# Dividing the softmax behind the product with v instead of ahead of it

## The chip, the core and the metric

The kernel runs on one core of a Trainium2 chip. The metric is the device time of one execution in microseconds, the median of several runs; less is better. The core has five engines that matter here, each with a queue of its own: TensorE (PE in the profile; PEld is its weight load), VectorE (DVE), ScalarE (ACT), GpSimd (POOL) and SyncE (SP), which issues the transfers. TensorE writes PSUM, eight banks of 128 x 512 float32; everything else lies in SBUF.

## What is computed

A two-layer encoder over 512 tokens of width 1024. Each layer is a half-step feed-forward block, a token mixer and another feed-forward block. The mixer makes q, k, v and u by one projection, runs windowed attention (8 heads of 64, 2 key/value heads, blocks of 128 queries) beside a state-space branch, normalizes both results and projects them out. The part that is changed is the end of the attention:

```
s = q k^T / 8 + bias, masked to |i - j| <= 128
m = max(max(s), sink);  p = exp(s - m)
denom = sum(p) + exp(sink - m)
p = p / denom
o = p v
attn = o;  rms_norm(attn) goes into the output projection
```

## The kernel before

Activations are kept with channels on the partitions and the 512 tokens in columns. Products of float32 data are made as three products of rounded parts (`mm3`, L214 to L218): high by high, high by low, low by high. ScalarE rounds the high part of each weight chunk (L199), VectorE, for some chunks GpSimd, subtracts to get the low part (L202).

The mixer (L762) is a list of small steps in the order of `ORDER` (L42 to L46), emitted one after the other. Attention has eight units, a block n of 128 queries with a key/value head kv; unit 0 is (0, 0), unit 1 is (0, 1), and so on. For each unit:

- `as` (a_scores, L954): the scores of four heads, bias and maximum on VectorE (L971), exp with its row sums on ScalarE (L978), the sink's term (L979).
- `an` (a_norm, L982): VectorE adds the sink's term (L988), takes the reciprocal (L989) and multiplies the four heads' p by it, one instruction per head (L993). Queries lie on the partitions here, so the factor is one number per partition.
- `ao` (a_out, L995): TensorE turns p by transposes of 128 x 128, four to a PSUM bank (L1001); VectorE (L1004) or ScalarE (L1006) copies each bank out.

For each block n there is then `pv` (a_pv, L1011): the product with v, one product for each key block and kv (L1016); a float32 product shows as two records in the trace. The two kv use different halves of the array's columns and write different partitions of one bank o. Behind it VectorE multiplies o by the gain of the norm (L1025, result f), ScalarE rounds f to its high part (L1027) and squares o (L1028), VectorE makes the low part (L1030), and GpSimd, for n = 3 VectorE, adds up the squares (L1032, L1033). The second output projection (`wa`, from L1148, by `wout`) needs all four blocks' high and low parts; the rstd of the norm (`rstd_a`, L329) needs the sums of squares. The first output projection, of the state-space branch, is the steps `ws0` to `ws7`, twelve products of 128 x 512 each; its sums are made by L1069 and added to x by L1071. The feed-forward block behind the mixer rounds x by L281 and L287 first.

The list ends with `... as7 ws6 an7 ao7 ao6 pv2 ws7 pv3`. Emission sets the dependences, but not alone the order within an engine's queue: the kernel asks that queues be planned when it is compiled (`TCKW`, L38), and the trace shows steps out of the order of the list. The preparation of the second layer's state-space tables (`s5_steps`, L518, in the trace L456 to L641) is emitted behind the first mixer, and some of it runs during the mixer's end.

PSUM banks are handed out in turn, the one that was given back first being next (`bank`, L146). SBUF slots of 128 x 512 come from 16 blocks of four (`slot`, L101).

Of the kernel before, what the change touches and what calls it, by code (L numbers as in the profile page):

```python
# [11 lines left out]
AF = mybir.ActivationFunctionType  # L12
# [17 lines left out]

# column indices in the table of per-partition gains
GC_FFN1, GC_MIX, GC_ATT, GC_SSM, GC_FFN2, GC_BGLU, GC_L = 0, 8, 16, 20, 24, 32, 36
# [7 lines left out]
N_CONST = 640  # L40
# order of the parts of the token mixer (see Emit.mixer)
ORDER = """  # L42
# [3 lines left out]
""".split()  # L46
# weight chunks of the mixer, by halves, whose low parts GpSimd makes
POOL_SPLIT = {("u", 0, 0), ("u", 0, 1), ("u", 2, 0), ("q", 0, 0), ("q", 0, 1), ("q", 2, 1), ("glu", 0, 1),
              ("ws", 0, 1), ("ws", 4, 0), ("wa", 0, 1), ("wa", 4, 1)}
# low parts of q, by head of the group and half, that GpSimd makes  # L50
POOL_Q = ((2, 1), (3, 1))
# tiles of the output whose sums in the mixer VectorE makes, of the first and of the second product
ADD_V = ((0, 7), (5, 7))
# tiles of x, by first and number, as they are loaded
STARTX = ((0, 1), (1, 1), (2, 2), (4, 2), (6, 2))


def weight_chunks():
    """Chunks of stationary blocks in the order of their use: (kind, args, columns)."""
    out = []  # L60
    for l in range(L):
        for which in (0, 1):
            if which == 1:
                out += [("u", (l, 0), 2048), ("u", (l, 2), 2048), ("kv", (l,), 2048),
                        ("q", (l, 0), 2048), ("q", (l, 2), 2048)]
                out += [("glu", (l,), 2048), ("ws", (l, 0), 2048), ("ws", (l, 4), 2048),
                        ("wa", (l, 0), 2048), ("wa", (l, 4), 2048)]
            for f0, nf in FGROUPS:
                for f in range(f0, f0 + nf):
                    out.append(("gu", (l, which, f), 2048))  # L70
                for dp in range(4):
                    out.append(("dn", (l, which, f0, nf, dp), 2 * nf * P))
    return out


class Emit:
# [22 lines left out]

# [1 line left out]
    def slot(self, n=1, r=False):  # L101
# [56 lines left out]

# [1 line left out]
    def set_bg(self, gen, steps, points):  # L160
        """Spread gen, of about so many steps, over so many points of the main work."""
        self.bg = gen
        self.bg_at, self.bg_n, self.bg_rate = 0, 0, steps / points
# [13 lines left out]

# [1 line left out]
    def w_load(self, upto):  # L179
# [39 lines left out]

# [1 line left out]
    def const(self, n):  # L221
# [5 lines left out]
    def setup(self, st):  # L227
        """Constants, the input, and the first chunk of weights, in the order in which the first products want them."""
        I, V, S, SP, Gp = self.I, self.V, self.S, self.SP, self.G
# [44 lines left out]

# [1 line left out]
    def x_hi(self, d, st):  # L276
        """The rounded part of h = x * gain for tile d."""
        if d % 4 == 0:
            st["blk"] += [self.slot(4, True), self.slot(4, True)]
        hi, lo = (x[:, (d % 4) * T:(d % 4 + 1) * T] for x in st["blk"][-2:])  # L280
        self.S.activation(hi.bitcast(F32R), self.x[d], AF.Copy, scale=self.gains[:, st["g"] + d:st["g"] + d + 1])  # L281
        st["h"].append((hi, lo))

    def x_lo(self, d, st):
        """The rest of h."""
        hi, lo = st["h"][d]
        self.V.scalar_tensor_tensor(lo.bitcast(F32R), self.x[d], self.gains[:, st["g"] + d:st["g"] + d + 1], hi,  # L287
                                    op0=ALU.mult, op1=ALU.subtract)
# [6 lines left out]
    def x_acc(self, d, st, eng):  # L295
        """The running sum of squares."""
        if d:
# [25 lines left out]
    def rstd_a(self, acc, n, w=T):  # L323
        """Column sums of acc -> 1/sqrt(mean + eps), as columns of 128 tokens."""
        V = self.V
# [15 lines left out]
    def rstd_b(self, s, w=T):  # L341
        """The columns as one row of tokens, the same on each partition."""
        b = self.bank()
# [7 lines left out]

# [1 line left out]
    def ffn(self, st, after, tail=None):  # L353
# [65 lines left out]

# [1 line left out]
    def bias_steps(self):  # L421
# [27 lines left out]

# [1 line left out]
    def cmul(self, eng, o, a, b, t, conj=False):  # L451
        """o = a * b (or conj(a) * b), pairs of (re, im)."""
        M, A, B = ALU.mult, ALU.add, ALU.subtract
# [9 lines left out]
    def exp_parts(self, x, w, R):  # L463
        """exp(x) = 2**k * (1 + em): returns (em, 2**k) as tiles of width w."""
        V = self.V
# [18 lines left out]
    def sincos(self, th, w, R):  # L484
        """(cos(th) - 1, sin(th)) with th reduced to [-pi, pi] and then halved."""
        V = self.V
# [31 lines left out]
    def s5_steps(self, l):  # L518
# [60 lines left out]
        yield  # L579
        # powers 0..8  # L580
        tmp = self.slot()
# [20 lines left out]

        # input matrices, as they are and turned back by one chunk
        def g16(x):
# [13 lines left out]
        yield  # L618
        # phasors of 1, 2, 4, .. chunks, backward ones conjugate, of modulus 1
        rho = R()  # L620
# [8 lines left out]
        for k in range(5):  # L629
# [13 lines left out]
            yield  # L643
        # tables over the chunks, 16 groups at a time
        for hf in range(2):
# [34 lines left out]
        yield  # L680
        # output maps, input maps and the taps inside a chunk, 4 groups at a time
        ks = self.slot(3)
# [70 lines left out]

# [1 line left out]
    def proj(self, w, m, h, bank):  # L755
# [6 lines left out]
    def mixer(self, l, st, after):  # L762
# [5 lines left out]

        # u, with the tokens of a chunk apart: (j, c) for t = 8 c + j
        ud = self.dram.tile([4, P, T], F32, name=f"ud{l}")  # L770
# [34 lines left out]

        # state-space pieces, a quarter of the groups at a time
        tabs, Y = {}, {}
# [62 lines left out]
        def s_out(q):  # L870
# [14 lines left out]
            if q % 2 == 0:  # L885
                Y[gh] = [self.slot(), self.slot()]
            # rows (group parity, c); columns (j, group pair, channel)
            for jh in range(2):
# [58 lines left out]

        # attention
        ga = self.gains[:, gl + GC_ATT:gl + GC_ATT + 4]
# [32 lines left out]
        def a_norm(n, kv):  # L982
            k0, k1 = at[n]["k"]
            nk = (k1 - k0) * P
            sm = at[n]["sm"]
# [3 lines left out]
            V.reciprocal(den[:, c4], den[:, c4])  # L989
            for i in range(4):  # L990
                hd = kv * 4 + i
                p = at[n]["p"][kv][:, i * T:i * T + nk]
                V.tensor_scalar(p, p, den[:, hd:hd + 1], None, op0=M)  # L993

# [16 lines left out]
        def a_pv(n):  # L1011
            k0, k1 = at[n]["k"]
            o = self.bank()
            for kb in range(k0, k1):
# [3 lines left out]
            for kv in range(2):  # L1018
                self.free(*at[n][kv])
            # rows (kv, dh); columns (head of the group, token)  # L1020
            if not abuf:
                abuf.extend([self.slot(4, True), self.slot(4, True)])
            cs = slice(n * T, (n + 1) * T)
            f, q = self.slot(), self.slot()
            V.tensor_tensor(out=f.rearrange("p (i t) -> p i t", i=4), in0=o.rearrange("p (i t) -> p i t", i=4),  # L1025
                            in1=ga.rearrange("p (i o) -> p i o", o=1).to_broadcast([P, 4, P]), op=M)
            S.copy(abuf[0][:, cs].bitcast(F32R), f)  # L1027
            S.activation(q, o, AF.Square)  # L1028
            self.bfree(o)
            V.tensor_tensor(out=abuf[1][:, cs].bitcast(F32R), in0=f, in1=abuf[0][:, cs], op=B)  # L1030
            eng = V if n == 3 else Gp
            eng.tensor_tensor(out=q[:, 0:256], in0=q[:, 0:256], in1=q[:, 256:512], op=A)  # L1032
            eng.tensor_tensor(out=acc_a[:, n * P:(n + 1) * P], in0=q[:, 0:P], in1=q[:, P:2 * P], op=A)  # L1033
            self.free(f, q, at[n]["sm"])

        # back to channels on the partitions, and the activation
        z = [None] * 4
# [121 lines left out]
    def final(self, st):  # L1159
        """The last two tiles of the last product, the last norm and the output, half of the tokens at a time."""  # L1160
        V, S, Gp = self.V, self.S, self.G
# [68 lines left out]

# [1 line left out]
def _tiles(w, cols):  # L1232
    """w: (K, N); the 128-column blocks of w[:, cols] as [128, m, k, 128]."""
    k = w.shape[0] // P
    m = len(cols) // P
    return w[:, cols].reshape(k, P, m, P).transpose(1, 2, 0, 3)
# [42 lines left out]
def _bucket(rel):  # L1279
    """Bucket of each relative distance (a constant of the shapes)."""  # L1280
    half, exact = 16, 8
# [81 lines left out]
```

## Time and profile before

| | us |
|---|---|
| median of 3 runs | 1935.28 |
| lowest and highest run | 1933.37, 1935.31 |
| span of the profiled execution | 1932.9 |
| PE busy in the span | 1859.6 (96%) |
| DVE, ACT, POOL busy | 1138.8, 627.4, 698.0 |

The span runs from the first to the last instruction of one profiled execution; that execution's own time is not listed apart from its span. The median of the runs is 2.4 us more than the span, for what lies around it.

How to read the profile: a line of a view names the engine, the source line, the operation and the tiles. A timeline gives start and length of merged runs of the same instruction, and in brackets how long the engine had waited and for whom. The distance between two starts on TensorE is what an instruction costs there, since the records of neighbours overlap.

### The profile page before, as it was taken

To read this page: it belongs to the slowest core of one execution; us is meant where nothing else is said; L and a number is where in the kernel's file an instruction comes from. 1 tells how busy PE (TensorE), PEld (TensorE's weight loads), DVE (VectorE), ACT (ScalarE), POOL (GpSimd) and SP (SyncE) were. 2 spreads that over 40 slices of the span, in tenths; PEclk is the share of its full clock that TensorE was granted. 3 is DMA by queue.
4 is the path that set the end of the run, shared out by engine and by line. 5 is a ranking of instruction groups with operands and counts; after the bars stand their busy time and mean duration, and the time that the engine had idled before them with its cause. 6 is when DMAs were issued, how large, how long until landed. Compare 5 with 4: busy or idle time off the path is not lost. (4 is left out here: it accounts for less than half of the span.)

```text
span 1932.9 us, 23810 instructions
## 1 busy us (share of the span) xinstructions
PE 1859.6 (96%) x9416; PEld 1506.9 (78%) x9416; DVE 1138.8 (59%) x1747; ACT 627.4 (32%) x955; POOL 698.0 (36%) x586
## 2 busy tenths in 40 slices
PE   8999999996999999999999999999969999999997
PEld 6888888875667888888878888888747678888886
DVE  8645545569889634355674453436797773434435
ACT  5223223321743323223332222224227342222223
POOL 2049999235133015093483351103341330201102
PEclk9999999997999999999999999999979999999998
DMA  5533434576111233233333244424640122232321
GB/s 201 164 120 121 160 124 157 160 239 214 50 67 46 107 109 120 99 131 115 108 136 111 99 135 129 138 93 154 219 170 23 51 83 107 88 106 80 109 97 45
DMA packets 86233, 231.13 MB, mean 120 GB/s; under 512 B 31160, under 2 KB 38504, under 8 KB 70376
## 3 DMA queue, kind: packets, MB, share of 16 engines
q1 hardware_dynamic: 84888, 228.51, 35.0%
q8 instruction: 74, 1.21, 0.3%
q10 hardware_dynamic: 1232, 1.09, 0.2%
q14 instruction: 39, 0.32, 0.1%
HBM read 201.11 MB, written 34.75 MB: 122 GB/s over the span
## 5 line engine op out<-in xcount | busy, mean ns | idle before, releaser
L217 PE MATMUL psum<-blk,whi 128*128 128x512 f32 (+1 forms) x2446 | 952.9, 390 | 7.7 <-DVE blk L287 7.6
L216 PE MATMUL psum<-blk,whi 128*128 128x512 f32 (+1 forms) x2446 | 952.4, 392 | 7.5 <-ACT blk L281 6.3
L218 PE MATMUL psum<-blk,wlo 128*128 128x512 f32 (+1 forms) x2446 | 950.6, 389 | 0.9 <-DVE wlo L202 0.7
L217 PEld LDWEIGHTS psum<-blk,whi 128*128 128x128 f32 x2446 | 460.4, 188 | 106.2 <-DVE blk L287 12.8
L216 PEld LDWEIGHTS psum<-blk,whi 128*128 128x128 f32 x2446 | 460.8, 188 | 104.9 <-ACT blk L281 6.5
L218 PEld LDWEIGHTS psum<-blk,wlo 128*128 128x128 f32 x2446 | 460.3, 188 | 96.2 <-DVE wlo L202 1.1
L199 ACT CAST whi<-raw 128x1024 fp32r<-128x1024 f32 (+1 forms) x310 | 303.4, 1027 | 680.1 <-PE psum L217 466.6
L202 DVE TENSOR_TENSOR wlo<-raw,whi 128x1024 fp32r<-128x1024 f32 (+1 forms) x288 | 417.5, 1484 | 38.1 <-ACT whi L199 28.2
L385 DVE TENSOR_TENSOR blk<-psum,blk 128x512 f32<-128x512 f32 x88 | 60.6, 691 | 346.0 <-PE psum L218 343.6
L411 POOL TENSOR_TENSOR xtile<-xtile,blk 128x512 f32<-128x512 f32 x64 | 91.1, 1424 | 375.8 <-DVE blk L409 358.4
L409 DVE SCALAR_TENSOR_TENSOR blk<-psum,blk 128x512 f32<-128x512 f32 x94 | 64.9, 690 | 213.5 <-PE psum L218 203.2
L384 ACT ACTIVATE blk<-blk 128x512 f32<-128x512 f32 x88 | 55.3, 632 | 301.8 <-DVE blk L382 296.8
L701 POOL TENSOR_TENSOR blk<-blk,blk 128x512 f32<-128x512 f32 x64 | 85.4, 1346 | 92.0 <-PE psum L714 51.4
L382 DVE TENSOR_TENSOR blk<-psum,blk 128x512 f32<-128x512 f32 x88 | 60.2, 688 | 88.2 <-PE psum L218 85.4
L299 POOL TENSOR_TENSOR blk<-blk,blk 128x512 f32<-128x512 f32 x29 | 45.0, 1553 | 155.1 <-ACT blk L292 154.3
L202 POOL TENSOR_TENSOR wlo<-raw,whi 128x1024 fp32r<-128x1024 f32 x22 | 61.1, 2785 | 106.6 <-ACT whi L199 65.8
L702 POOL TENSOR_TENSOR blk<-blk,blk 128x512 f32<-128x512 f32 x64 | 85.8, 1343 | 27.5 <-PE psum L714 14.3
L704 POOL TENSOR_TENSOR blk<-blk,blk 128x512 f32<-128x512 f32 x49 | 80.2, 1642 | 2.4
L389 DVE TENSOR_TENSOR blk<-blk,blk 128x512 fp32r<-128x512 f32 x88 | 75.4, 859 | 0.7 <-ACT blk L388 0.7
L287 DVE SCALAR_TENSOR_TENSOR blk<-xtile,consts,blk 128x512 fp32r<-128x512 f32 x48 | 57.1, 1205 | 11.0 <-ACT blk L281 11.0
L1071 POOL TENSOR_TENSOR xtile<-xtile,blk 128x512 f32<-128x512 f32 x24 | 33.2, 1404 | 70.2 <-DVE blk L1069 63.7
L299 POOL TENSOR_TENSOR blk<-blk 128x512 f32<-128x512 f32 x13 | 20.5, 1574 | 99.0 <-ACT blk L292 98.8
(234 smaller groups left out, 1337.5 us busy)
## 6 DMA issues: line engine op xcount, KB each, us to landing
raw<-w SPq DMA_DIRECT2D x123, 1024.0 KB, 4.8
raw<-w SPq DMA_DIRECT2D x32, 896.0 KB, 4.6
fd<-blk SPq DMA_DIRECT2D x32, 256.0 KB, 2.8
ed<-blk SPq DMA_DIRECT2D x32, 256.0 KB, 3.4
blk<-ed SPq DMA_DIRECT2D x32, 256.0 KB, 6.3
blk<-fd SPq DMA_DIRECT2D x32, 256.0 KB, 5.2
tb<-blk SPq DMA_DIRECT2D x12, 512.0 KB, 2.9
blk<-tb SPq DMA_DIRECT2D x24, 256.0 KB, 5.8
```

What stands on the lines that cost most here:

```text
L199: self.S.copy(hi[:, c], raw[:, c])
L202: eng.tensor_tensor(out=lo[:, c], in0=raw[:, c], in1=hi[:, c].bitcast(F32), op=ALU.subtract)
L216: t.matmul(out, wh, xh, start=start, stop=False)
L217: t.matmul(out, wh, xl, start=False, stop=False)
L218: t.matmul(out, wl, xh, start=False, stop=stop)
L299: eng.tensor_tensor(out=acc, in0=acc, in1=sq, op=ALU.add)
L389: V.tensor_tensor(out=lo.bitcast(F32R), in0=s, in1=hi, op=ALU.subtract)
L409: V.scalar_tensor_tensor(t, ps, 0.5, R, op0=ALU.mult, op1=ALU.mult)
L411: (V if last else self.G).tensor_tensor(out=self.x[d], in0=self.x[d], in1=t, op=ALU.add)
L701: Gp.tensor_tensor(out=full(o), in0=mat(a), in1=pwo(w, 0), op=M)
L702: Gp.tensor_tensor(out=full(t), in0=mat(b), in1=pwo(w, 1), op=M)
L704: Gp.tensor_tensor(out=o, in0=o, in1=t, op=sg)
```

## The change

`a_norm` keeps the sum and the reciprocal, and no longer multiplies p. `a_out` turns the undivided p. `a_pv` first spreads the reciprocals: ScalarE copies the eight columns of block n to a tile rd, in which each number stands 64 times side by side; four transposes put them into a bank db, where rows are (kv, channel) and columns are (head, token); ScalarE copies the bank back to rd. Behind the product VectorE multiplies o by rd into rd, and the product with the gain is made from rd, by GpSimd for n = 0, 1, 2 and by VectorE for n = 3. The square is now emitted ahead of the rounding of f. Nothing else is changed (the rest of the diff takes comments out).

```
 def a_norm(n, kv):
-    k0, k1 = at[n]["k"]
-    nk = (k1 - k0) * P
     sm = at[n]["sm"]
     c4 = slice(kv * 4, kv * 4 + 4)
     den, t = sm[:, 16:24], sm[:, 24:32]
     V.tensor_tensor(out=den[:, c4], in0=den[:, c4], in1=t[:, c4], op=A)
     V.reciprocal(den[:, c4], den[:, c4])
-    for i in range(4):
-        hd = kv * 4 + i
-        p = at[n]["p"][kv][:, i * T:i * T + nk]
-        V.tensor_scalar(p, p, den[:, hd:hd + 1], None, op0=M)
 def a_pv(n):
     k0, k1 = at[n]["k"]
+    db, rd = self.bank(), self.slot()
+    S.copy(rd.rearrange("p (i k c) -> p i k c", i=4, k=2),
+           at[n]["sm"][:, 16:24].rearrange("p (k i o) -> p i k o", k=2, o=1).to_broadcast([P, 4, 2, 64]))
+    for i in range(4):
+        TE.transpose(db[:, i * P:(i + 1) * P], rd[:, i * P:(i + 1) * P], self.ident)
+    S.copy(rd, db)
+    self.bfree(db)
     o = self.bank()
...
     f, q = self.slot(), self.slot()
-    V.tensor_tensor(out=f.rearrange("p (i t) -> p i t", i=4), in0=o.rearrange("p (i t) -> p i t", i=4),
-                    in1=ga.rearrange("p (i o) -> p i o", o=1).to_broadcast([P, 4, P]), op=M)
+    eng = V if n == 3 else Gp
+    V.tensor_tensor(out=rd, in0=o, in1=rd, op=M)
+    self.bfree(o)
+    eng.tensor_tensor(out=f.rearrange("p (i t) -> p i t", i=4), in0=rd.rearrange("p (i t) -> p i t", i=4),
+                      in1=ga.rearrange("p (i o) -> p i o", o=1).to_broadcast([P, 4, P]), op=M)
+    S.activation(q, rd, AF.Square)
     S.copy(abuf[0][:, cs].bitcast(F32R), f)
-    S.activation(q, o, AF.Square)
-    self.bfree(o)
     V.tensor_tensor(out=abuf[1][:, cs].bitcast(F32R), in0=f, in1=abuf[0][:, cs], op=B)
-    eng = V if n == 3 else Gp
     eng.tensor_tensor(out=q[:, 0:256], in0=q[:, 0:256], in1=q[:, 256:512], op=A)
     eng.tensor_tensor(out=acc_a[:, n * P:(n + 1) * P], in0=q[:, 0:P], in1=q[:, P:2 * P], op=A)
-    self.free(f, q, at[n]["sm"])
+    self.free(f, q, rd, at[n]["sm"])
```

## Rows read from the trace of the kernel before

**Rows 1.** The page: busy us of each engine (share of the span) xinstructions.
```profile
PE 1859.6 (96%) x9416; PEld 1506.9 (78%) x9416; DVE 1138.8 (59%) x1747; ACT 627.4 (32%) x955; POOL 698.0 (36%) x586
```
**Rows 2.** Stretches: us, busy PE PEld DVE ACT POOL (xinstructions), PEclk, DMA, GB/s.
```profile
510.00:520.00 10.00, 10.00 (x39) 6.48 (x38) 7.49 (x20) 9.00 (x18) 1.04 (x1) 1.00 0.00 0
...
1510.00:1520.00 10.00, 10.00 (x47) 6.68 (x49) 8.04 (x27) 3.92 (x12) 2.56 (x2) 1.00 0.01 2
1520.00:1530.00 10.00, 8.95 (x43) 4.49 (x40) 8.29 (x10) 4.24 (x7) 3.63 (x3) 1.00 0.29 105
```
**Rows 3.** TensorE's waits, whole span: line waited for, us in total, times, longest.
```profile
PE psum L882 <- DMA blk<-td: 17.6, 2, 9.2
...
PE psum L216 <- ACT blk L1027: 1.2, 2, 0.7
```
**Rows 4.** Groups by line and shape, the removed multiplies: busy us, mean ns.
```profile
L993 DVE TENSOR_SCALAR blk<-blk,blk 128x384 f32<-128x384 f32 x32 | 13.2, 470 | 0.1
...
L993 DVE TENSOR_SCALAR blk<-blk,blk 128x256 f32<-128x256 f32 x32 | 10.8, 399 | 0.3
```
**Rows 5.** The same view, nearest rows to the added operations.
```profile
L1071 POOL TENSOR_TENSOR xtile<-xtile,blk 128x512 f32<-128x512 f32 x24 | 33.2, 1404 | 70.2 <-DVE blk L1069 63.7 <-DVE blk L988 4.6 <-ACT blk L292 1.9
...
L1001 PE MATMUL psum<-consts,blk 128*128 128x128 f32 x160 | 22.1, 279 | 0.0
...
L1006 ACT COPY blk<-psum 128x512 f32<-128x512 f32 x20 | 11.8, 595 | 23.3 <-PE psum L1001 23.3
...
L1025 DVE TENSOR_TENSOR blk<-psum,consts 128x512 f32<-128x512 f32 x8 | 5.5, 682 | 1.4 <-PE psum L1016 1.4
```
**Rows 6.** Timeline, TensorE, first layer, pv0: start us, length, line.
```profile
519.62 0.66 PE L1001 MATMUL psum<-consts,blk 128*128 128x128 f32 x4
520.20 1.07 PE L1016 MATMUL psum<-blk,blk 128*64 128x512 f32 x2
...
522.80 0.66 PE L1001 MATMUL psum<-consts,blk 128*128 128x128 f32 x4
523.21 0.42 PE L968 MATMUL psum<-blk 128*128 128x384 f32 x1
```
**Rows 7.** Timeline, TensorE, second layer, end of the attention.
```profile
1515.01 1.07 PE L1016 MATMUL psum<-blk,blk 128*64 128x512 f32 x2
1516.01 0.50 PE L216 MATMUL psum<-blk,whi 128*128 128x512 f32 x1
...
1518.96 1.94 PE L1016 MATMUL psum<-blk,blk 128*64 128x512 f32 x8
1520.83 1.09 PE L1001 MATMUL psum<-consts,blk 128*128 128x128 f32 x8
1521.86 1.07 PE L1016 MATMUL psum<-blk,blk 128*64 128x512 f32 x2
...
1526.28 1.07 PE L1016 MATMUL psum<-blk 128*64 128x512 f32 x2
...
1528.78 1.65 PE L216 MATMUL psum<-blk,whi 128*128 128x512 f32 x6 [0.74 <-ACT blk L1027]
```
**Rows 8.** Timeline, VectorE, the same end of the attention.
```profile
1516.16 1.95 DVE L993 TENSOR_SCALAR blk<-blk,blk 128x256 f32<-128x256 f32 x4
...
1527.39 0.69 DVE L1025 TENSOR_TENSOR blk<-psum,consts 128x512 f32<-128x512 f32 x1 [0.90 <-PE psum L1016]
```
**Rows 9.** Timeline, ScalarE, the same end of the attention.
```profile
1515.53 0.19 ACT L979 ACTIVATE blk<-blk 128x4 f32<-128x4 f32 x1
...
1528.11 0.62 ACT L1027 CAST blk<-blk 128x512 fp32r<-128x512 f32 x1 [1.85 <-DVE blk L1025]
```
**Rows 10.** Timeline, VectorE, first layer, x being rounded behind the mixer.
```profile
597.94 1.27 DVE L632 SCALAR_TENSOR_TENSOR blk<-blk 128x32 f32<-128x32 f32 x1
```
**Rows 11.** TensorE's waits from 570 to 625 us, first layer: total, times, longest.
```profile
PE psum L217 <- DVE blk L287: 4.6, 3, 1.9
```
**Rows 12.** TensorE's waits from 1515 to 1570 us, second layer.
```profile
PE psum L217 <- DVE blk L287: 2.2, 2, 1.4
```

## The prediction

> **What bounds the kernel now.** I read the busy shares first: TensorE is busy for 1859.6 of 1932.9 us, VectorE for 59% [rows 1]. So a microsecond counts only where TensorE does more or less, or waits. The second view is the list of TensorE's waits [rows 3]. The largest, 17.6 us, is for the loads of the state-space taps ahead of the attention; the change touches nothing there. No row of the list names the multiplies that go away (L993): nothing that TensorE multiplies by waits for them directly. Third, the stretches: where the attention runs, TensorE is busy for the full 10.00 of 10 us, at the full clock (granted 1.00, 2.4 GHz), and only in the last stretch does that fall to 8.95 [rows 2]. So the attention is bound by TensorE up to its end. Its end is a chain: last product with v, L1025 on VectorE, L1027 on ScalarE, first product of the output projection. Its wait shows as 0.74 us in the second layer [rows 7], 1.2 us in both [rows 3].
>
> **What the change removes.** 64 multiplies of VectorE, 13.2 + 10.8 = 24.0 us [rows 4]. They lie beside TensorE's work, so they are worth nothing by themselves; the cover is TensorE's own full queue. What can be worth something is that p is ready to be turned earlier. In the second layer's last unit exp is done at 1515.53 + 0.19 = 1515.7 [rows 9], the multiplies end at 1516.16 + 1.95 = 1518.1 [rows 8]: 2.4 us.
>
> **What it adds to TensorE.** Eight groups of four transposes, four in each layer. The nearest row is the same instruction (L1001). Start to start, four of them take 523.21 - 522.80 = 0.41 us where work of full array width follows [rows 6], and eight take 1521.86 - 1520.83 = 1.03 [rows 7]. Wedged between two products with v they cost more: 520.20 - 519.62 = 0.58 [rows 6], and the way out of the product ahead comes on top. Two pairs of halves and the way out take 1520.83 - 1518.96 = 1.87, one half alone and the way out 1516.01 - 1515.01 = 1.00 [rows 7]; a half alone takes as long as a pair, since the two run side by side, so a pair is 0.87 and the way out 0.13. A group is thus 0.41 at best and 0.58 + 0.13 = 0.71 at worst; all eight 3.3 to 5.7 us. I take 0.71 for pv0, since turns already stand between its products [rows 6], and 0.41 elsewhere.
>
> That the wedge is dearer agrees with a rule of the Trainium skill (TensorEngine Tiling (Array Packing), Key Properties): changing the tiling mode drains TensorE. It speaks against this change, which brings full-width transposes to a product of half-width tiles; by the rule all eight groups would be at the dear end, by the rows only those that stand wedged.
>
> **What it adds elsewhere.** ScalarE gets two copies per block, 16 x 0.595 us = 9.5 us by L1006 [rows 5]. The copy with repeated elements has no row; I bound it by 0 (hidden) and by L1006's 0.595 on a queue that others wait for, and take it as hidden except where ScalarE is full: 9.00 of 10 us around 515 us of the first layer [rows 2], just ahead of pv0. Behind the second copy, which waits for the transposes, stand the exps and copies of the next units; TensorE has the products of `ws` to do meanwhile. VectorE gets eight multiplies at 0.682 us [rows 5] in the place of L1025, with the same wait. Six gain products go to GpSimd, 6 x 1.404 = 8.4 us by L1071 [rows 5]. GpSimd is busy for only 2.56 and 3.63 us of the last two stretches [rows 2]; block 2's product has more than 3 us before block 3's is due, so it is hidden, and the low part and sums of squares behind it with it. If the cover were gone, it would add 1.4 us a layer. No DMA is added or moved; SP's queue keeps its order.
>
> For block 3 VectorE multiplies twice. The chain from the last product to the projection is 1528.78 - (1526.28 + 1.07) = 1.43 us now [rows 7]. One more VectorE step is 1528.11 - 1527.39 = 0.72 with its hand-over [rows 8, 9]. The square (0.6 us) runs on ScalarE beside that step. New chain: 2.15 us.
>
> **The end of the attention again.** Now the twelve products of `ws7` run at 1516.01, ahead of the turns of units 7 and 6 at 1520.83 [rows 7], though the list has the turns first: they were not ready. Behind that, halves of the products wait alone for their turns (1515.01 and 1521.86, two records each, 1.00 us). With p ready at 1515.7 the turns can go first. From 1515.01: 16 turns 2.06, three pairs of pv2 1.87 + 0.87 = 2.74, `ws7` 1518.96 - 1516.01 = 2.95, two pairs of pv3 1.87, two added groups 0.82, and 0.30 for one more way in (0.58 - 0.41) and out: 10.74, to 1525.75. Plus the chain of 2.15: the projection starts at 1527.9 in place of 1528.78, 0.9 us earlier although two groups and the longer chain are in it.
>
> **Sum.** Per layer +0.71 (pv0) + 0.41 (pv1) - 0.88 (end) = +0.24; two layers +0.5 us. 1932.9 + 0.5 = 1933.4, and with the 2.4 us by which the runs' median exceeds the span, 1935.8 us. That is no change that can be told: about 0.2% (3.9 us) is what a measurement of this kernel can tell.
>
> **Rival 1, slower: TensorE pays in full.** The queues keep their order, `ws7` ahead of the turns. Then nothing is won at the end: per layer four groups at 0.41 to 0.71 and 0.72 of longer chain, 2.36 to 3.56, in both 4.7 to 7.1 us: 1940.0 to 1942.4. For it: TensorE is full [rows 2], so every added product is time. At the end of a layer the reordering is to win 0.88 + 0.82 + 0.72 = 2.4 us gross; the change is measurably slower once 1.7 us of that fail in each layer (3.9 - 0.5 = 3.4 in both). Against: the turns have only p to wait for. One bank more per block, and two more copies where ScalarE is full, push the same way.
>
> **Rival 2, faster: VectorE's relief reaches the stage behind.** Behind the mixer TensorE waits for L287, where x is rounded: 4.6 us in the first layer [rows 11], where pieces of the next layer's preparation stand between, such as L632 with 1.27 us [rows 10], and 2.2 us in the second [rows 12], where there are none. VectorE is relieved by 24.0 - 5.4 + 4.1 = 22.7 us in all. If the preparation moves forward into that room, 4.6 falls to 2.2, -2.4 us; if pv0's two halves also close up, one time of 1.00 us per layer goes, -2.0; and pv0's group is then a cheap one, -0.6. With the forecast's +0.5 that is -4.5: 1930.8. Against: the preparation starts late because of its loads and its room as well, and the freed time lies mostly ahead of it.
>
> **Rival 3: the change does nothing that TensorE sees.** The groups fill small holes and the chain is covered: 1935.3. It can't be told from the forecast, and I count it there.
>
> **How the numbers follow.** Forecast and rival 3: 0.50. Rival 1: 0.29. Rival 2: 0.21. Faster by over 0.2% is below 1931.4, slower above 1939.2, so these are the three chances. The range reaches from rival 2's time to the middle of rival 1, 1930.8 to 1941.5, leaving out about half of rival 2 and a quarter of rival 1. The forecast's own range is 1932 to 1939.
>
> **What would show it.** In the trace after: 32 more transposes that take 0.41 us by fours, 0.58 where wedged; turns of units 7 and 6 ahead of `ws7` in both layers; the projection's start 2.1 us behind the last product; VectorE's busy time some 23 us less, ScalarE's some 9 us more, GpSimd's some 8 us more; waits for L287 about as before. I am wrong if the turns stay behind `ws7`, if TensorE waits in the attention for a bank or for ScalarE, or if slots that are handed out in another order delay the loads of the second layer.

## The result: 13 us slower, and where they are

The changed kernel takes 1948.0 us (median, 1946.4 to 1948.1) against 1934.8 us for the kernel before (median of the runs taken beside it), a ratio of 1.0067 (95% interval 1.0054 to 1.0080). The forecast was 1935.8, its range ended at 1941.5: the change is slower, by more than rival 1 allowed. The profiled span grew from 1932.9 to 1944.6 us, by 11.7.

The page of the changed kernel, busy us of each engine:

```profile
PE 1866.1 (96%) x9448; PEld 1513.1 (78%) x9448; DVE 1124.7 (58%) x1685; ACT 636.1 (33%) x971; POOL 706.7 (36%) x592
```

Against [rows 1] TensorE is busy for 6.5 us more, of which the 32 transposes are 3.6 (below), and VectorE's busy time falls by 14.1 us. TensorE's waits in the whole span (line waited for, us in total, times, longest):

```profile
PE psum L882 <- DMA blk<-td: 17.1, 2, 9.5
...
PE psum L216 <- ACT blk L1033: 8.2, 2, 4.2
PE psum L217 <- DVE blk L287: 6.6, 6, 2.5
PE psum L218 <- DVE wlo L202: 2.4, 2, 1.3
```

One row has grown by much: the output projection's first product (L216) waits for the cast of the attention (L1033 now, L1027 in [rows 3]), 8.2 us in place of 1.2. The wait for a low part of the weights (L202) went from 0.7 to 2.4. To see how much of the loss lies ahead of that product and how much behind it, I cut the span in four at two products of each layer: the last transposes of the state-space branch (L943) and the first product of the output projection. The rows that set the cuts, first of the kernel before (for layer 2 the projection is in [rows 7]), then of the changed one:

```profile
433.04 0.66 PE L943 MATMUL psum<-consts,blk 128*128 128x128 f32 x4 [1.75 <-DVE blk L860]
...
575.28 1.65 PE L216 MATMUL psum<-blk,whi 128*128 128x512 f32 x6 [0.47 <-ACT blk L1027]
...
1386.73 0.66 PE L943 MATMUL psum<-consts,blk 128*128 128x128 f32 x4 [1.75 <-DVE blk L860]
```
```profile
432.41 0.66 PE L943 MATMUL psum<-consts,blk 128*128 128x128 f32 x4 [1.75 <-DVE blk L860]
...
578.75 2.93 PE L216 MATMUL psum<-blk,whi 128*128 128x512 f32 x6 [4.16 <-ACT blk L1033]
...
1391.98 0.66 PE L943 MATMUL psum<-consts,blk 128*128 128x128 f32 x4 [1.75 <-DVE blk L860]
...
1536.36 2.64 PE L216 MATMUL psum<-blk,whi 128*128 128x512 f32 x6 [4.03 <-ACT blk L1033]
```

The same cuts in the kernels told of below, each stretch as the difference from the kernel before:

| us | attention, layer 1 | projection 1 to attention 2 | attention, layer 2 | projection 2 to the end |
|---|---|---|---|---|
| before | 142.24 | 811.45 | 142.05 | 404.12 |
| changed | +4.1 | +1.8 | +2.3 | +4.1 |
| changed, TensorE kept busy (a_fill) | +5.4 | -1.7 | +2.9 | +0.8 |
| changed, `ws7` last (a_ws7) | +2.6 | +1.9 | +0.8 | +0.2 |
| changed, no GpSimd beside it (a_act) | +4.6 | +3.1 | +0.8 | +2.6 |
| before without the multiplies (b_nodiv) | +2.4 | +2.4 | +0.3 | -0.3 |

So half of the changed kernel's loss (1.8 + 4.1 of 11.7 us) is behind the wait, in stretches in which the change itself has no instruction. The end of its second attention, TensorE's timeline:

```profile
1522.28 0.60 PE L1012 MATMUL psum<-consts,blk 128*128 128x128 f32 x4
1522.81 2.79 PE L1018 MATMUL psum<-blk,blk 128*64 128x512 f32 x12
1525.54 0.50 PE L216 MATMUL psum<-blk,whi 128*128 128x512 f32 x1
...
1529.30 0.60 PE L1012 MATMUL psum<-consts,blk 128*128 128x128 f32 x4
...
1531.74 0.59 PE L1018 MATMUL psum<-blk 128*64 128x512 f32 x1
```

and beside it VectorE, GpSimd and ScalarE:

```profile
1529.52 0.68 DVE L1072 TENSOR_TENSOR blk<-psum,blk 128x512 f32<-128x512 f32 x1
1530.35 1.23 DVE L202 TENSOR_TENSOR wlo<-raw,whi 128x1024 fp32r<-128x1024 f32 x1
1531.49 2.83 DVE L1074 TENSOR_TENSOR xtile<-xtile,blk 128x512 f32<-128x512 f32 x1
1534.25 0.68 DVE L1028 TENSOR_TENSOR blk<-psum,blk 128x512 f32<-128x512 f32 x1
1534.96 0.69 DVE L1030 TENSOR_TENSOR blk<-blk,consts 128x512 f32<-128x512 f32 x1
...
1531.34 2.44 POOL L202 TENSOR_TENSOR wlo<-raw,whi 128x1024 fp32r<-128x1024 f32 x1 [2.02 <-ACT whi L199]
...
1529.27 1.99 ACT L199 CAST whi<-raw 128x1024 fp32r<-128x1024 f32 x2 [0.32 <-PE psum L217]
...
1535.69 0.62 ACT L1033 CAST blk<-blk 128x512 fp32r<-128x512 f32 x1
```

The last product with v ends at 1531.74 + 0.59 = 1532.3. VectorE could multiply it then, and does so at 1534.25: ahead of it in the queue stand what follows `ws7`, its sum (L1072), a low part (L202) and the sum into x (L1074). The last takes 2.83 us beside GpSimd's L202, which ran until 1533.78. Then come the two steps of the new chain, and the projection starts 4.0 us behind the last product. In layer 1 the last product ends at 573.69 + 0.59 = 574.3, the projection starts 4.5 us later, and a 128x32 step of the next layer's preparation plays the same part:

```profile
573.69 0.59 PE L1018 MATMUL psum<-blk 128*64 128x512 f32 x1
...
573.01 1.22 DVE L202 TENSOR_TENSOR wlo<-raw,whi 128x1024 fp32r<-128x1024 f32 x1
574.39 2.08 DVE L468 TENSOR_SCALAR blk<-blk 128x32 f32<-128x32 f32 x1 [0.16 <-DMA blk<-s5p]
...
576.59 0.68 DVE L1028 TENSOR_TENSOR blk<-psum,blk 128x512 f32<-128x512 f32 x1
...
573.51 2.92 POOL L202 TENSOR_TENSOR wlo<-raw,whi 128x1024 fp32r<-128x1024 f32 x1 [2.49 <-ACT whi L199]
```

**Theory 1**, which the runs were to test: the loss is this wait and its sequel. VectorE's queue and the collision with GpSimd lengthen the chain by 2 us a layer, and in the wait TensorE's clock falls. **Theory 2**: TensorE pays for the spreading all along the attention (rival 1, enlarged). **Theory 3**: the earlier p alone brings the loss, through the order at the end; the spreading is beside the point.

### The profile page after: what moved, and what is told of

Read it like the earlier page. It is cut to its first block, busy times and chain, and to the rows that moved or that the text cites. A ratio compares the mean times of both kernels' runs of the same rounds, so it can differ in the third digit from the quotient of the medians.

```text
span 1944.6 us, 23832 instructions
## 1 busy us (share of the span) xinstructions
PE 1866.1 (96%) x9448; PEld 1513.1 (78%) x9448; DVE 1124.7 (58%) x1685; ACT 636.1 (33%) x971; POOL 706.7 (36%) x592
## 4 chain that ended last, share of the span: by engine, by line
PE 82%; DVE 10%; POOL 3%; issue 2%; DMA 2%; ACT 1%; SPq 1%; DVEq 0%; POOLq 0%; ACTq 0%
PE psum L216 25%; PE psum L217 25%; PE psum L218 25%; DVE wlo L202 2%; DVE blk L856 1%; DVE blk L287 1%; DVE blk L857 1%; PE psum L882 1%; POOL blk L701 1%; PE psum L969 1%; PE psum L995 1%; POOL blk L704 1%; PE psum L1018 1%; PE psum L968 1%; PE psum L732 1%
## 5 line engine op out<-in xcount | busy, mean ns | idle before, releaser
L216 PE MATMUL psum<-blk,whi 128*128 128x512 f32 (+1 forms) x2446 | 956.6, 393 | 14.3 <-ACT blk L1033 8.2
L216 PEld LDWEIGHTS psum<-blk,whi 128*128 128x128 f32 x2446 | 462.5, 189 | 115.1 <-ACT blk L1033 9.1
L199 ACT CAST whi<-raw 128x1024 fp32r<-128x1024 f32 (+1 forms) x310 | 303.4, 1027 | 660.1 <-PE psum L217 456.7
L202 DVE TENSOR_TENSOR wlo<-raw,whi 128x1024 fp32r<-128x1024 f32 (+1 forms) x288 | 419.7, 1491 | 27.6 <-ACT whi L199 17.3
L202 POOL TENSOR_TENSOR wlo<-raw,whi 128x1024 fp32r<-128x1024 f32 x22 | 61.5, 2803 | 105.5 <-ACT whi L199 85.0
L287 DVE SCALAR_TENSOR_TENSOR blk<-xtile,consts,blk 128x512 fp32r<-128x512 f32 x48 | 56.2, 1187 | 10.7 <-ACT blk L281 10.7
L1074 POOL TENSOR_TENSOR xtile<-xtile,blk 128x512 f32<-128x512 f32 x24 | 35.2, 1488 | 64.8 <-DVE blk L1072 63.0
```

The costliest lines, as they stand in the source:

```text
L199: self.S.copy(hi[:, c], raw[:, c])
L202: eng.tensor_tensor(out=lo[:, c], in0=raw[:, c], in1=hi[:, c].bitcast(F32), op=ALU.subtract)
L216: t.matmul(out, wh, xh, start=start, stop=False)
```

## The experiments

**a_fill: TensorE kept busy in the wait.**

```
+            if n == 3:
+                fb = self.bank()
+                for i in range(4):
+                    TE.matmul(fb, vt[:, 0:P], at[n][i % 2][-1], start=True, stop=True)
+                self.bfree(fb)
```

> The changed kernel with four products more (128x512, all rows, their result unused) put behind the last product with v of each layer, where TensorE otherwise waits 4 us for the cast of the attention. They bring TensorE some 3.4 us of work into that wait, and add nothing that the chain waits for.
> Theory 1, its part on the clock (after the wait the products take 0.43 us in place of 0.23 until the clock is back, 1.8 to 2.7 us a layer): the granted clock stays at 1.00 behind the end of the attention, and the time falls by 3 to 5 us, to 1943 to 1945, although TensorE does 6.8 us more.
> If the slow products have another cause: 1948, or above it by what of the four products sticks out of the wait.

Measured: 1941.1 us (before 1935.1), 6.9 below the changed kernel with 8 products more in all. VectorE's sum into x still takes 2.84 us at the same place. What differs is the clock. Stretches of TensorE behind the projection's start (us, busy PE with its instructions, granted clock, DMA, GB/s), first the changed kernel, then a_fill:

```profile
578.70:585.00 6.30, 6.25 (x16) 0.55 0.54 204
1536.30:1541.00 4.70, 4.64 (x14) 0.64 0.34 145
```
```profile
580.90:587.20 6.30, 6.26 (x28) 1.00 0.55 207
1535.60:1540.30 4.70, 4.67 (x21) 1.00 0.30 120
```

In the same 6.3 and 4.7 us it does 28 and 21 instructions in place of 16 and 14. At 0.23 us for a product that is 2.8 and 1.6 us. So behind the wait the granted clock is at its lower level, 1.2 GHz, and the first products pay for it. The two later stretches of the table fall by 3.5 and 3.4 us. What of that is above 2.8 and 1.6 lies further on, where x is rounded and its sums are made. The waits for low parts (L202, 2.4 us in layer 1 of the changed kernel) are gone there. In layer 2 the clock falls in both kernels behind a wait for L287 (2.6 and 2.5 us), but for 3.4 us here and for 6.8 in the changed kernel; by 0.43 us a product for 0.23, that is some 1.6 us (an estimate). Of theory 1, the part on the clock is shown.

**a_ws7: the cover put back.**

```
-an6 pv1 ws4 ws5 ao5 as7 ws6 an7 ao7 ao6 pv2 ws7 pv3
+an6 pv1 ws4 ws5 ao5 as7 ws6 an7 ao7 ao6 pv2 pv3 ws7
```

> The changed kernel with its last two steps in the other order: the last block's products with v are emitted ahead of ws7, not behind it. Then ws7 (3 us of TensorE) lies in the wait for the chain, and its sum on VectorE stands behind the last product's multiply and not ahead.
> Theory 1: the wait of 4 us falls below 1 us in both layers, the clock stays up, and the time falls by 6 to 9 us, to 1939 to 1942; what is left over the kernel before is the transposes and the plain length of the chain.
> Theory 2 (TensorE pays for the spreading all along): the end gets shorter by no more than 2 us a layer, and the time stays at 1944 or above.

Measured: 1938.2 us, 9.8 below the changed kernel; 1.0018 (1.0009 to 1.0026) of the kernel before. The list of waits has no row for the cast any more. The end of layer 2, TensorE and then VectorE and ScalarE:

```profile
1529.77 1.02 PE L1018 MATMUL psum<-blk 128*64 128x512 f32 x2
1530.72 0.50 PE L216 MATMUL psum<-blk,whi 128*128 128x512 f32 x1
...
1533.71 1.17 PE L216 MATMUL psum<-blk,whi 128*128 128x512 f32 x4
```
```profile
1530.89 0.69 DVE L1028 TENSOR_TENSOR blk<-psum,blk 128x512 f32<-128x512 f32 x1 [1.63 <-PE psum L1018]
...
1535.77 2.89 DVE L1074 TENSOR_TENSOR xtile<-xtile,blk 128x512 f32<-128x512 f32 x1
...
1532.35 0.62 ACT L1033 CAST blk<-blk 128x512 fp32r<-128x512 f32 x1
```

The edit does two things at once. The multiply comes right behind the last product, so the chain is back at the length that I had forecast (1530.79 to 1532.97, 2.2 us), and `ws7` (from 1530.72, 3 us) covers it. Its sum still collides with GpSimd and takes 2.89 us, but behind the multiply, where nobody waits. So a_ws7 doesn't part the longer chain from the lost cover, but three quarters of the loss (9.8 of 13.2) are gone without touching the spreading, which speaks for theory 1 and against theory 2.

**a_act: no GpSimd beside VectorE.** For the half chunk `("wa", 4, 1)`, in place of the subtraction:

```
+self.S.mul(lo[:, c], raw[:, c], 2.0 ** -13)
```

> The changed kernel, in which the low part of one half chunk of the output projection's weights, which GpSimd makes in 2.4 to 2.9 us while VectorE does its last work ahead of the final multiply, is not made: ScalarE writes a small multiple of the weights in its place, so that GpSimd does nothing there. (The low part is left out of the products, and the output with it.) The queue of VectorE ahead of the final multiply keeps the sum of ws7 in layer 2, and the preparation's first steps in layer 1.
> If the collision with GpSimd is what makes ws7's sum take 2.83 us and the 128x32 step 2.08 us: they take 0.69 and 0.2 us, the projection starts about 2 us earlier in each layer, the wait of 4.2 falls to 2 to 2.6 us, and the time falls by 4 us, to 1944; by up to 8, to 1940, if the clock then stays up.
> If they are slow for another reason: they stay above 2 us, and the time stays at 1947 to 1949.

Measured: 1945.7 us, 2.4 below the changed kernel, short of the 4 expected. VectorE in layers 1 and 2:

```profile
576.41 0.18 DVE L468 TENSOR_SCALAR blk<-blk 128x32 f32<-128x32 f32 x1 [0.27 <-DMA blk<-s5p]
...
577.32 0.63 DVE L1028 TENSOR_TENSOR blk<-psum,blk 128x512 f32<-128x512 f32 x1
...
1533.55 0.68 DVE L1074 TENSOR_TENSOR xtile<-xtile,blk 128x512 f32<-128x512 f32 x1
1534.78 0.69 DVE L1028 TENSOR_TENSOR blk<-psum,blk 128x512 f32<-128x512 f32 x1 [0.55 <-ACT blk L1013]
```

The two slow steps are at their plain length, 0.18 and 0.68 us, the same instructions on the same shapes: the collision made them slow. It is shown as the cause of the length, not as the whole of the wait. The waits for the cast became 2.9 and 2.5 us, because seven small steps (L468 to L574) now stand ahead of the multiply in layer 1, and the multiply waits 0.55 us for ScalarE in layer 2, whose queue got the added work. Behind the 2.9 the clock fell again, behind the 2.5 it stayed at 1.00.

**a_fill_act: both.**

> The changed kernel with both of two earlier edits: four products more behind the last product with v (1941.1 by itself) and GpSimd's half of the output projection's low part left out, with a small multiple of the weights in its place (1945.7 by itself). That part is left out of the products and of the output.
> Theory 1, if the wait and the clock are two separate parts: the collision's 2 us a layer are now covered by the four products, so little is left for the second edit: 1939 to 1941.
> If the four products helped in another way than by the clock, both gains add in full: 6.9 + 2.4 from 1948, 1938 to 1939.

Measured: 1943.1 us, 2 above a_fill alone (1941.1), and outside both expectations. No wait for the cast is left. The wait for x being rounded (L287) takes 9.2 us in all here (7.2 in a_fill), and behind one of them, in layer 2, the clock is low for 6.8 us as in the changed kernel, not for 3.4. Why these waits grew I didn't settle; taking out a wait that is already covered won nothing.

**b_nodiv: the earlier p alone.** From the kernel before:

```
-            for i in range(4):
-                hd = kv * 4 + i
-                p = at[n]["p"][kv][:, i * T:i * T + nk]
-                V.tensor_scalar(p, p, den[:, hd:hd + 1], None, op0=M)
```

> The kernel before without the 64 multiplies of p, and nothing in their place: the division of the softmax is left out, and so is its effect on the output. No spreading, the chain at the end keeps its one VectorE step. p is ready early, as in the changed kernel.
> Theory 1: the turns go ahead of ws7 and the end gains 1 to 2 us a layer, but ws7's sum or a piece of the preparation can then stand ahead of the last product's multiply on VectorE, which gives some back: 1932 to 1936, and the wait for the cast of the attention is above the 0.7 us of before where such an instruction stands ahead.
> Theory 3 (the earlier p alone brings the loss, by the order of the work at the end): 1941 or above, with waits of about 4 us as in the changed kernel.
> Theory 2: 1930 to 1935, nothing is lost without the spreading.

Measured: 1938.7 us, 1.0015 (1.0006 to 1.0024) of the kernel before: taking 24 us off VectorE and adding nothing makes the kernel 3.6 us slower. Layer 1, TensorE, VectorE and GpSimd:

```profile
576.89 2.92 PE L216 MATMUL psum<-blk,whi 128*128 128x512 f32 x6 [2.61 <-ACT blk L1023]
...
573.42 1.96 DVE L468 TENSOR_SCALAR blk<-blk 128x32 f32<-128x32 f32 x1 [0.28 <-DMA blk<-s5p]
...
572.43 2.92 POOL L202 TENSOR_TENSOR wlo<-raw,whi 128x1024 fp32r<-128x1024 f32 x1 [2.79 <-ACT whi L199]
```

The same collision ahead of the last multiply, a wait of 2.6 us, and a granted clock of 0.54 in the 6.3 us behind it. The time lies between what theories 1 and 2 expected (up to 1936) and theory 3 (from 1941). In layer 2 the sum into x came out early enough, the wait is 1.1 us and the clock stays up. So theory 3 holds in part: the early p moves `ws7`, and that can cost a wait and the clock without any spreading. The step more in the chain makes it worse, and in both layers.

**b_ws7 and b_nodiv_ws7: the same exchange without the change.** Both have the edit of a_ws7, on the kernel before and on b_nodiv.

> The kernel before with its last two steps in the other order: the last block's products with v ahead of ws7. Here p is late, so ws7 was filling the wait for it.
> Theory 1 (what ws7 covers decides): ws7 now covers the chain's wait (1.2 us in all), but the turns, for which TensorE is 2 us early in each layer, lose their cover: 1935 to 1939, 0 to 4 us above the kernel before.
> Theory 2 (order at the end doesn't matter for the loss): 1933.5 to 1935.5.

> The kernel before without the 64 multiplies of p (the division of the softmax is left out), with ws7 behind the last products with v.
> Theory 1 and theory 3: p is early, ws7 covers the chain, nothing waits at the end and the clock stays up: against the same kernel with ws7 ahead (1938.7) it falls by 4 to 7 us, to 1932 to 1935. What the changed kernel with the same order takes above it is the price of the spreading: 4 to 6 us by the transposes' 0.43 us for four and what they disturb.
> Theory 2: the spreading costs 10 us and more, so this one stands at 1928 or below.

Measured: 1935.6 (1.0002, 0.9993 to 1.0011) and 1938.9 us. Neither tests what it was meant to, also where the time fell into a stated range (b_ws7). In their traces `ws7` still runs ahead of the last products with v: the list doesn't bind the queues, which are planned when the kernel is compiled, and only for the changed kernel did the plan follow it. In b_nodiv_ws7 layer 1 even waits 4.0 us for the cast, with no spreading in the program. I had expected the price of the spreading from the difference of a_ws7 and b_nodiv_ws7; that stays out.

**b_spread: the spreading alone.** The added copy, four transposes and copy ahead of each block's products, in the kernel before; nothing uses them.

> The kernel before, with its division kept, plus the spreading alone: the copy of one over the sums, the four transposes and the copy out of the bank stand ahead of each block's products with v, and nothing uses what they give. The multiplies of p stay, so p is ready as late as before, ws7 stays ahead of the last turns, and the chain at the end keeps its one VectorE step.
> Theory 1 (the loss of 13.2 us sits at the end of the attention: the longer chain, an instruction ahead of it on VectorE, and the clock that falls in the wait; the spreading costs TensorE only its 32 transposes): +3.3 to +5.7 us, so 1938 to 1940.5 against 1934.8, no wait of 4 us for the cast of the attention.
> Theory 2 (TensorE pays for the spreading all along the attention, by transposes, banks and ScalarE's copies): +10 us or more, 1945 or above.

Measured: 1947.9 us, +12.8: theory 2's number and not theory 1's. The runs spread from 1944.7 to 1953.2, and the profile is of the slowest. TensorE at the first products with v of layer 1, and the stretch behind it:

```profile
527.37 0.79 PE L216 MATMUL psum<-blk,whi 128*128 128x512 f32 x1 [2.72 <-DVE blk L971]
```
```profile
527.30:543.60 16.30, 16.23 (x48) 0.50 0.07 28
```

That product reads nothing that L971 makes. L971 reads scores out of a bank, so I take it that the product waits for a bank, of which the spreading holds one more; no run tests that. Then the clock is down for 16 us, some 7 to 8 us of loss (an estimate, by 0.43 for 0.23). In layer 2 the same wait is 2.1 us, and the clock is down for 5 us behind it. Other waits grew with them: 2.7 us in all for L287, 2.0 for the cast, 3.1 ahead of products with v for copies of turned p. The changed kernel's list has no wait for L971, so this is not what it paid. But it shows that the spreading can cost far more than its transposes when p is late.

**a_ws7_2t: the transposes twice.** From a_ws7, `for i in (0, 1, 2, 3, 0, 1, 2, 3)`.

> The changed kernel with ws7 behind the last products with v (1938.2), in which each of the eight groups of four transposes that spread one over the sums runs twice. 32 transposes more, nothing else.
> If TensorE pays for each in full: 8 groups by 0.41 to 0.71 us, +3.3 to +5.7, so 1941.5 to 1944.
> If they fit into holes: 1938 to 1939.
> Theory 2, by which the spreading costs 10 us through TensorE: 1945 or above.

Measured: 1948.3 us, +10.1, above all that was expected of transposes, and again theory 2's number. The trace puts it elsewhere. In layer 2, where `ws7` still covers the chain, the attention's stretch grew by 1.1 us for four groups (142.9 to 144.0), so 0.3 us a group, less than the 0.41 that I had said. In layer 1 the plan put ten products of `ws7` ahead of the last products with v, and two waits came back, the second behind a 128x32 step of 2.35 us:

```profile
581.73 1.66 PE L216 MATMUL psum<-blk,whi 128*128 128x512 f32 x6 [2.77 <-ACT blk L1033]
585.37 0.50 PE L217 MATMUL psum<-blk,whi 128*128 128x512 f32 x1 [1.98 <-DVE blk L1034]
```

**a_one and a_one_ws7: a chain one step shorter.** GpSimd makes rd times the gain ahead of the products, VectorE makes f from it at once:

```
+            Gp.tensor_tensor(out=rg..., in0=rd..., in1=ga..., op=M)
...
+            V.tensor_tensor(out=f, in0=o, in1=rg, op=M)
             V.tensor_tensor(out=rd, in0=o, in1=rd, op=M)
```

> The changed kernel with a chain that is one step shorter: GpSimd multiplies the spread one over the sums by the gain ahead of the products with v, so that VectorE multiplies the product once and the cast can follow; the product without the gain, for the squares, is made behind it. With it the sum of ws7 comes to stand ahead of VectorE's low part of the weights in layer 2, and so ahead of GpSimd's.
> Theory 1 (the loss is the wait at the end): the step saves 0.7 us a layer, and layer 2 loses its slow sum as well, 2 us; the waits for the cast fall to about 3.4 and 1.5 us, the clock stays up in layer 2 at least, and the time falls by 3.5 to 6 us, to 1942 to 1944.5.
> Theory 2: 1946 to 1948.

> The changed kernel with both the shorter chain and ws7 behind the last products with v.
> Theory 1: ws7 covers the chain already, so the shorter chain has nothing left to give: 1937.5 to 1939, as with ws7 alone (1938.2); GpSimd's product ahead of each block stands in nobody's way.
> Theory 2 expects nothing of it either; a time below 1934 would say that the chain still costs where it isn't seen as a wait.

Measured: 1958.6 and 1957.7 us, 10 us above the changed kernel, and 20 above a_ws7. Both miss by far. TensorE in layer 1 of a_one:

```profile
529.05 1.12 PE L1012 MATMUL psum<-consts,blk 128*128 128x128 f32 x4 [3.69 <-ACT blk L1009]
```

Here the first block's transposes stand on TensorE ahead of `ws0`. They wait for ScalarE's copy (L1009), which stands behind a table load of 1.28 us and four exps. In the changed kernel the copy is as late, but `ws` products stand in between and nobody waits. In a_one the cast is waited for longer than in the changed kernel, 6.2 and 4.3 us: GpSimd's new product stands behind its L202, and in layer 2 VectorE's multiply waits 3.23 us for it. So the edit lengthened what it was to shorten, and the two runs show nothing on the chain's length. They show the price of a wait in TensorE's queue: 8.5 us in all for the copy, and the clock.

**a_ws7_wa: the other collision.** From a_ws7, `("wa", 0, 1)` taken out of `POOL_SPLIT`.

> The changed kernel with ws7 behind the last products with v (1938.2), and with the low part of the output projection's first half chunk on VectorE in place of GpSimd. In the changed kernel that GpSimd work runs beside VectorE's 128x4 step at the first products with v of layer 1, which takes 2.34 us, and TensorE waits 0.7 us behind it.
> If that collision is what is left at pv0: the 128x4 step takes 0.15 us, the wait goes, 1 to 2 us less, 1936.5 to 1937.5.
> If VectorE's 1.2 us more stand in its place: 1938 to 1939.

Measured: 1938.4 us, the same as a_ws7. The 128x4 step still takes 2.34 us, beside another GpSimd L202: I had taken the wrong half chunk for its partner. It tells nothing on pv0.

No version that I ran beats the kernel before.

## Why the prediction was wrong

**What held.** The turns went ahead of `ws7` or into it in both layers, and the halves of the products ran in pairs. The groups of transposes cost 0.33 to 0.59 us start to start (0.53 in front of pv2, 1522.28 to 1522.81), 3.6 us for all eight against 3.9 in the forecast. From the last state-space transposes to the end of the last product with v, layer 2 took 1532.3 - 1392.0 = 140.3 us, against 1527.35 - 1386.73 = 140.6 before ([rows 7] for the end): 0.3 less, where the forecast had 0.5 less (0.71 + 0.41, and 1.60 by which the last product's end was to come earlier). Layer 1 took 574.3 - 432.4 = 141.9 against 140.6, so 1.2 more. In both a part is chance: the wait for the taps' load, which the change doesn't touch, was 1.6 us shorter in layer 2 (7.6 for 9.2) and 1.1 longer in layer 1 (9.5 for 8.4). I take from it only that TensorE's own work in the attention is not where most of the loss lies. ScalarE's and GpSimd's busy times grew by 8.7 us each, as forecast; VectorE's fell by 14 and not 23, which I did not trace. GpSimd's gain product takes 1.04 us and not 1.40, and is hidden.

In layer 1 a small wait came up at pv0, where I had feared one for ScalarE. It is for VectorE: the scores' product behind pv0 waits 0.70 us for a copy of turned p (L998), which stands behind a 128x4 step that took 2.34 us beside GpSimd:

```profile
519.65 2.34 DVE L974 TENSOR_SCALAR blk<-blk 128x4 f32<-128x4 f32 x1
...
519.43 2.54 POOL L202 TENSOR_TENSOR wlo<-raw,whi 128x1024 fp32r<-128x1024 f32 x1 [25.86 <-ACT whi L199]
```

**The step that failed** is "The end of the attention again", and in it "plus the chain of 2.15". I moved `ws7` behind the turns on TensorE and left everything that hangs on it where it was. Its products free the weights' tiles: ScalarE's cast of the next chunk (L199) waits for them, then come the two halves of the low part on VectorE and GpSimd (L202), and its own two sums. All of these moved with it, from 6 us ahead of the last product to beside it. The kernel before has the same collision, in the two rows that I had not read:

```profile
1521.07 2.84 DVE L1071 TENSOR_TENSOR xtile<-xtile,blk 128x512 f32<-128x512 f32 x1
...
1520.92 2.44 POOL L202 TENSOR_TENSOR wlo<-raw,whi 128x1024 fp32r<-128x1024 f32 x1 [3.74 <-ACT whi L199]
```

There the multiply (1527.39 in [rows 8]) came 3.5 us after it and found VectorE idle. So the chain of 2.15 us became 4.0 in layer 2 and 4.5 in layer 1: 1.9 and 2.3 us more.

The rule for this stands in the Trainium skill (SBUF — State Buffer, "SBUF: two separate sides"): VectorE and GpSimd share a pair of ports as an exclusive lock. A VectorE instruction that runs in a two-port mode or has two SBUF inputs, and a GpSimd instruction that reads SBUF, exclude each other: whoever comes second is blocked for the whole instruction of the first. The rows agree: the sum into x, which has two such inputs, ended 0.54 us behind the end of GpSimd's L202 (1534.32, 1533.78), where the sum alone takes 0.68 (a_act). The 128x32 and 128x4 steps have one input and were held as well; no row shows the mode that they run in. A step that reads PSUM was not held, in the kernel before:

```profile
519.20 0.62 DVE L971 CUSTOM_DVE_ANT_0 blk<-psum,biast,consts 128x384 f32<-128x384 f32 x1
...
518.96 2.54 POOL L202 TENSOR_TENSOR wlo<-raw,whi 128x1024 fp32r<-128x1024 f32 x1 [24.83 <-ACT whi L199]
```

So the last multiply, which reads PSUM, lost its time in VectorE's queue, behind the step that was held.

**The term that was missing** is the clock. The prediction read the granted clock of 1.00 and asked of no wait what it does to the clock. Behind the waits of 4.2 and 4.0 us it was low, at 2.8 and 1.6 us, 4.4 in both (a_fill). With the chain's 4.2 us, the waits for low parts (2.4 against 0.7) and the 0.7 at pv0 that is 11.0 us on top of the forecast's 0.5, against 11.7 measured in the span. That the sum comes so close is in part luck, for it leaves out what partly cancels: layer 1's attention (1.2 us more, 0.7 of it counted), the waits for L287, 1.0 us less in all, and the clock, which falls once more behind one of these in either kernel, for 3.4 us in layer 1 before and for 6.8 in layer 2 after (some 1.6 us more, an estimate).

**The rivals.** Rival 1 had the sign, by another mechanism: the queues did not keep their order, and the transposes, 3.6 us, are the smaller part of the 11.7. Its price of 4.7 to 7.1 us has no wait and no clock in it. Its condition, the order kept and p late, is b_spread, which came to +12.8 by the waits for L971 and the clock. Of rival 2 one half came: the wait for L287 behind the mixer fell from 4.6 to 2.6 us in layer 1 [rows 11], but in layer 2 it rose from 2.2 to 3.2 [rows 12], so it gave 1.0 and not 2.4. That the early p can do harm by itself (b_nodiv, +3.6) was on no list.

**What stays open.** a_ws7 is 3.1 us above the kernel before, in the profile 5.1. Its attention stretches hold 3.4 of these, about as much as the transposes cost. Of the 1.9 us behind the first projection some 1.2 are the clock (an estimate): behind a wait of 3.6 us for L287 it is low for 5.9 us, where the kernel before has two waits of 1.8 and 1.9 us and is low for 3.4. Why the wait came in one piece is open. So is whether b_spread waits for a bank, why the waits for L287 grew in a_fill_act, and where the rest of a_ws7_2t's loss in layer 1 lies beside its two waits.

## What to carry to other kernels

When a step moves on TensorE, list what waits for it and what frees by it on the other engines, and place those anew: a queue that was idle at the end of a chain need not be idle after the move. Price a wait of TensorE twice, by its length and by the products that run at the lower clock behind it, and keep some independent products to put into it. Work taken off an engine that bounds nothing is no gain, and by the order that it changes it can be a loss.

## What the runs showed of the hardware

- VectorE steps that read SBUF alone and begin 0.1 us or more behind the start of GpSimd's 128x1024 subtraction last until that ends, the 128x512 ones some 0.5 us longer: 128x512 2.83 us in place of 0.68, 128x32 2.08 in place of 0.18, 128x4 2.34 in place of 0.15. A step that reads PSUM is not held: 0.62 us (L971, the kernel before), and 0.69 for the last multiply of b_nodiv's layer 2.
- Behind TensorE's waits of 4.2, 4.0, 2.9 (a_act), 2.7 (b_spread) and 2.6 us (b_nodiv), and of 2.1 in b_spread's layer 2, the granted clock was at the lower level, behind 2.8 (a_ws7_2t) and 2.5 us (a_act) it was not, so its length alone does not tell. A product of 128x512 then takes 0.43 us from start to start in place of 0.23. It was back after 6 us in the changed kernel's layer 1, after 4 in layer 2 and after 16 in b_spread.
